# A weighted sum over eight experts: engine code without a block, longer weight runs, and another split of the last eighteen tokens

## The chip, the cores and the metric

The kernel runs on one core of one Trainium2 chip. Its time is the device time of one execution in microseconds; below, "the time" is the median of three executions. One further execution was recorded by the hardware profiler, and all views come from that one.

A core has a tensor engine (PE; its weight loads are shown apart, as PEld), a vector engine (DVE), a scalar engine (ACT), GpSimd (POOL) and SyncE (SP), and 16 DMA engines that serve transfers issued from SP and from ACT. Engines wait for each other through semaphores. An on-chip tensor has 128 partitions.

## The reference

```
# expert_outputs: [16, 1024, 8, 512] float32      combine_weights: [16, 1024, 8] float32
weights = combine_weights[..., np.newaxis]
return np.sum(expert_outputs * weights, axis=2).astype(np.float32)
```

For each of 16,384 tokens, eight vectors of 512 numbers are scaled by eight weights and summed. 268 MB are read and 33.6 MB are written, so each byte that is read is used once.

## The kernel before

Each of the 128 partitions works on 128 tokens of its own. "Token j" below means one token in every partition, so 128 tokens at once; its input is 2 MB and its output 0.25 MB.

**Layout.** The first 120 tokens of a partition come in 12 rounds of R = 10. In a round a partition holds ten neighbouring tokens, that is one block of 160 KB in memory, and the next partition has the next block. The last eight tokens (`x_l`, `w_l`, `o_l`) are eight neighbours per partition. `ring` holds the input of ten tokens on chip, `acc` ten results, `w_t` all weights, `w_c` the weights of the current round.

**The loop.** Rounds 0 to 10 (`ROUNDS` = 11, `LOOP` = 110 tokens) run in a hardware loop on DVE alone. In each pass DVE takes the three chunks of a round (4, 4 and 2 tokens); for each it waits for the copied weights (`w_set`), for the stores that free `acc` (`stored`) and for the load (`loaded`). Then it works on two tokens at a time: a scaled copy for term 0 (L226), and fused multiply-adds for terms 1 to 7 (L230), the two tokens taking turns so that no instruction follows directly on the one whose sum it needs. The last term of a token raises `done`. The argument `head_slot` of the loop sets at which place of an instruction fetch block the loop's first instruction lies.

**The tail.** The last 18 tokens (`TAIL`, j = 0 to 17; the last two are called a and b) are split between PE and DVE. ACT makes diagonal matrices from an identity and a weight (`diag`, L161), 32 of them ahead. PE multiplies such a matrix with a token's input and adds up terms 0 to 3 in one of eight PSUM banks (`ps`, L208). DVE adds terms 4 to 7, still two tokens at a time: its first instruction for a token reads `ps` and waits for `product`, the count of finished products; the others read `acc`.

**Queues.** SP issues all loads in order: weights (L114, L117), the loop's chunks (L122, each after `done` says that its place in `ring` is free), the tail's (L131: two tokens at a time, then single ones, and a and b in pieces of four, two and one term). After the last load SP issues the "held" stores of tokens 10 to 15, a and b (L137), each once DVE has done its tokens; at last it waits for all stores. ACT issues the stores of the loop (L178) and of tokens 0 to 9 (L191), copies weights and makes the diagonals.

**The block.** Every engine's code stands in a function of its own under one `nc.Block()`. The block's entry and its end (L110) are branches of every engine, and its end is a barrier of all engines; a second barrier of the surrounding program follows (L315).

Of the kernel before, what the change touches and what calls it, by code (L numbers as in the profile page):

```python
# [10 lines left out]
def kernel(  # L11
# [16 lines left out]
    nc = tc.nc  # L28
# [5 lines left out]
    P = 128  # L34
    R = 10
    T_P = T // P
    FULL = T_P // R
# [6 lines left out]
    PE_E = 4  # L44
    DIAGS = 8 * PE_E
    BANKS = 8

# [4 lines left out]
    x_r = x[0:cut].rearrange("(n p r) e d -> n p r e d", p=P, r=R)  # L52
    w_r = w[0:cut].rearrange("(n p r) e -> p n r e", p=P, r=R)
    o_r = o[0:cut].rearrange("(n p r) d -> n p r d", p=P, r=R)
    x_l = x[cut:T].rearrange("(p r) e d -> p r e d", r=LAST)
    w_l = w[cut:T].rearrange("(p r) e -> p r e", r=LAST)
    o_l = o[cut:T].rearrange("(p r) d -> p r d", r=LAST)

# [9 lines left out]


    tail_loads = [(j, 2, 0, E) for j in range(0, R, 2)]  # L70
    tail_loads += [(j, 1, 0, E) for j in range(R, TAIL - 2)]
    a, b = TAIL - 2, TAIL - 1
    tail_loads += [(a, 1, 0, 4), (b, 1, 0, 4), (a, 1, 4, 6), (b, 1, 4, 6)]
    tail_loads += [(a, 1, 6, 8), (b, 1, 6, 7), (b, 1, 7, 8)]

    tail_stores = [(0, 4), (4, 4), (8, 2)]
    held_stores = [(R, 6), (a, 1), (b, 1)]
# [15 lines left out]

    def x_tail(j, m, e0, e1):
        if j < R:
            return x_r[ROUNDS, :, j : j + m, e0:e1]
        return x_l[:, j - R : j - R + m, e0:e1]

    def o_tail(j, m):
        if j < R:  # L100
            return o_r[ROUNDS, :, j : j + m]
        return o_l[:, j - R : j - R + m]
# [5 lines left out]

    with tc.tile_critical(no_gpsimd_drain=True):  # L109
        with nc.Block() as block:  # L110

            @block.sync
            def _(sync):
                sync.dma_start(  # L114
                    out=w_t[:, 0 : FULL * R].rearrange("p (n r) e -> p n r e", r=R), in_=w_r
                ).then_inc(w_in, 16)
                sync.dma_start(out=w_t[:, FULL * R : T_P], in_=w_l).then_inc(w_in, 16)  # L117
                for n in range(ROUNDS):
                    for c, (r, m) in enumerate(CHUNKS):
                        if n:  # L120
                            sync.wait_ge(done, (n - 1) * R + r + m)
                        sync.dma_start(  # L122
                            out=ring[:, r : r + m], in_=x_r[n, :, r : r + m]
                        ).then_inc(loaded[c], 16)
                free = 0
                for k, (j, m, e0, e1) in enumerate(tail_loads):
                    if LOOP - R + j + m > free:
                        free = LOOP - R + j + m
                        sync.wait_ge(done, free)
                    r = j % R  # L130
                    sync.dma_start(  # L131
                        out=ring[:, r : r + m, e0:e1], in_=x_tail(j, m, e0, e1)
                    ).then_inc(tail_in[k], 16)
                for j, m in held_stores:
                    r = j % R
                    sync.wait_ge(done, LOOP + j + m)
                    sync.dma_start(out=o_tail(j, m), in_=acc[:, r : r + m]).then_inc(held_out, 16)  # L137
                sync.wait_ge(held_out, 16 * len(held_stores))
                for k in range(len(tail_stores)):
                    sync.wait_ge(tail_out[k], 16)  # L140

            @block.gpsimd
            def _(gpsimd):
                gpsimd.memset(ident, 0.0).then_inc(id_set, 1)  # L144
                gpsimd.affine_select(  # L145
                    out=ident,
                    in_=ident,
                    compare_op=mybir.AluOpType.not_equal,
                    fill=1.0,
                    base=0,  # L150
                    pattern=[[-1, P]],
                    channel_multiplier=1,
                ).wait_op(id_set, 1, "sem-ge").then_inc(id_set, 1)

            @block.scalar
            def _(scalar):
                def diags(j):

                    for e in range(PE_E):
                        k = j * PE_E + e  # L160
                        i = scalar.mul(  # L161
                            out=diag[:, k % DIAGS],
                            in_=ident,
                            mul=w_t[:, LOOP + j, e : e + 1],
                        ).then_inc(diag_set, 1)
                        if k >= DIAGS:
                            i.wait_op(product, k - DIAGS + 1, "sem-ge")

                scalar.wait_ge(w_in, 32)
                for n in range(ROUNDS + 1):  # L170
                    if n == ROUNDS:
                        scalar.wait_ge(id_set, 2)
                        for j in range(DIAGS // PE_E):
                            diags(j)
                    for c, (r, m) in enumerate(CHUNKS):
                        if n:
                            scalar.wait_ge(done, (n - 1) * R + r + m)
                            scalar.dma_start(  # L178
                                out=o_r[n - 1, :, r : r + m], in_=acc[:, r : r + m]
                            ).then_inc(stored[c], 16)  # L180
                        if n < ROUNDS:
                            scalar.copy(  # L182
                                out=w_c[:, r : r + m], in_=w_t[:, n * R + r : n * R + r + m]
                            ).then_inc(w_set[c], 1)
                ahead = DIAGS // PE_E
                for k, (j, m) in enumerate(tail_stores):
                    while ahead < min(TAIL, j + m + 6):
                        diags(ahead)
                        ahead += 1
                    scalar.wait_ge(done, LOOP + j + m)  # L190
                    scalar.dma_start(out=o_tail(j, m), in_=acc[:, j : j + m]).then_inc(  # L191
                        tail_out[k], 16
                    )
                while ahead < TAIL:
                    diags(ahead)
                    ahead += 1

            @block.tensor
            def _(tensor):
                for j in range(TAIL):  # L200
                    if j >= BANKS:
                        tensor.wait_ge(done, LOOP + j - BANKS + 1)
                    for e in range(PE_E):
                        k = j * PE_E + e
                        if e == 0 or load_of(j, e) != load_of(j, e - 1):
                            tensor.wait_ge(tail_in[load_of(j, e)], 16)
                        tensor.wait_ge(diag_set, k + 1)
                        tensor.matmul(  # L208
                            ps[:, j % BANKS],
                            lhsT=diag[:, k % DIAGS],  # L210
                            rhs=ring[:, j % R, e],
                            start=e == 0,
                            stop=e == PE_E - 1,
                        ).then_inc(product, 1)

            @block.vector
            def _(vector):
                def take(s, v):
                    vector.wait_ge(s, v).then_inc(s, -v)  # L219

                count = {}

                def term(r, e, first, weight, before):

                    if before is None:
                        i = vector.tensor_scalar_mul(  # L226
                            out=acc[:, r], in0=ring[:, r, e], scalar1=weight
                        )
                    else:
                        i = vector.scalar_tensor_tensor(  # L230
                            out=acc[:, r],
                            in0=ring[:, r, e],
                            scalar=weight,
                            in1=before,
                            op0=mult,
                            op1=add,
                        )
                    if e > first:
                        i.wait_op(step, count[r], "sem-ge")
                    if e < E - 1:  # L240
                        i.then_inc(step, 1)
                        count["all"] += 1
                        count[r] = count["all"]
                    else:
                        i.then_inc(done, 1)
                    return i

                for c in range(C):
                    vector.sem_inc(stored[c], 16)
                with nc.Fori(  # L250
# [69 lines left out]
```

## Time and profile before

| What | Value |
|---|---|
| time, median of three | 712.41 us (712.12 to 712.58) |
| the profiled execution: its own time, its span | 712.39 us, 710.5 us |
| DVE busy | 604.5 us (85%) |
| PE, PEld, ACT busy | 69.5, 28.4, 30.3 us |
| bytes moved, mean rate | 302.57 MB, 426 GB/s |
| one fused term of 128x512 on DVE | 745 ns |
| one diagonal on ACT, one PE pass | 388 ns, 637 ns (as recorded) |
| issue to landing of a tail load (L131), median | 36.6 us |

The span goes from the first recorded instruction to the last; the rest of the time lies around it. Busy time is that of an engine's own instructions; semaphore, branch and DMA-issuing instructions are not counted. Durations overlap where an engine is pipelined: a fused term is recorded with 745 ns, but six in a row take 4.06 us, and a matrix product of float32 shows as two passes. A row of the chain of waits names what released each step, followed back from the end.

### The profile page before, as it was taken

The numbers are of one execution on the slowest core, as the hardware profiler recorded it, in microseconds if no ns is written. First come the engines' busy times: TensorE is split into PE (matmuls) and PEld (weight loads), VectorE is DVE, ScalarE is ACT, GpSimd is POOL, SyncE is SP. The second block draws the span as 40 slices with busy tenths as digits, with TensorE's granted clock in tenths as the row PEclk, the third lists the DMA queues.
The fourth block names the chain that finished last, engine by engine and source line by source line (L and its number), as shares of the span: only waits on it lengthen the run. The fifth ranks groups of instructions, "written<-read, shape, count | busy, mean of one in ns | idle before, by whom it ended". The sixth has DMA issues, their size and how long they took to land. (4 is left out here: it accounts for less than half of the span.)

```text
span 710.5 us, 1687 instructions
## 1 busy us (share of the span) xinstructions
PE 69.5 (10%) x144; PEld 28.4 (4%) x144; DVE 604.5 (85%) x952; ACT 30.3 (4%) x106; POOL 0.7 (0%) x6
## 2 busy tenths in 40 slices
PE   0000000000000000000000000000000000567775
PEld 0000000000000000000000000000000000222322
DVE  0599899899899899899899899899899899954555
ACT  0000000000000000000000000000000140021200
POOL 0000000000000000000000000000000000000000
PEclk9999999999999999999999999999999999998998
DMA  9999999999999999999999999999999999999996
GB/s 381 421 420 461 410 422 438 452 405 467 409 427 437 457 405 462 404 439 429 455 415 448 415 436 439 438 421 443 445 408 456 422 447 410 424 441 425 429 425 247
DMA packets 14661, 302.57 MB, mean 426 GB/s; under 512 B 3136, under 2 KB 3136, under 8 KB 5568
## 3 DMA queue, kind: packets, MB, share of 16 engines
q1 hardware_dynamic: 9472, 271.06, 88.6%
q10 hardware_dynamic: 5184, 31.46, 10.5%
q14 instruction: 4, 0.03, 0.0%
q8 instruction: 1, 0.02, 0.0%
HBM read 268.96 MB, written 33.55 MB: 426 GB/s over the span
## 5 line engine op out<-in xcount | busy, mean ns | idle before, releaser
L230 DVE SCALAR_TENSOR_TENSOR acc<-ring,w_c,acc 128x512 f32<-128x512 f32 x770 | 514.7, 745 | 0.0
L208 PE MATMUL ps<-ring,diag 128*128 128x512 f32 x144 | 69.5, 637 | 632.2 <-DMA ring<-in_expert_outputs_dram 621.6
L226 DVE TENSOR_SCALAR acc<-ring,w_c 128x512 f32<-128x512 f32 x110 | 48.3, 481 | 64.5 <-DVEq L219 64.5
L208 PEld LDWEIGHTS ps<-ring,diag 128*128 128x128 f32 x144 | 28.4, 203 | 672.5 <-DMA ring<-in_expert_outputs_dram 624.1
L230 DVE SCALAR_TENSOR_TENSOR acc<-ring,w_t,ps 128x512 f32<-128x512 f32 x18 | 13.4, 746 | 37.4 <-PE ps L208 37.4
L230 DVE SCALAR_TENSOR_TENSOR acc<-ring,w_t,acc 128x512 f32<-128x512 f32 x54 | 36.5, 746 | 0.0
L182 ACT COPY w_c<-w_t 128x32 f32<-128x32 f32 (+1 forms) x33 | 6.8, 213 | 557.2 <-DVE acc L230 554.0
L161 ACT ACTIVATE diag<-ident,w_t 128x128 f32<-128x128 f32 x72 | 22.2, 388 | 84.6 <-PE ps L208 77.0
L182 ACT ACT_TABLE_LOAD x1 | 1.3, 1283 | 0.9 <-SPq L109 0.9
L145 POOL TENSOR_SCALAR_AFFINE_SELECT ident<-ident 128x128 f32<-128x128 f32 x1 | 0.3, 292 | 0.1
L144 POOL MEMSET ident<- 128x128 f32 x1 | 0.2, 204 | 0.5 <-SPq L109 0.5
L304 POOL MEMSET const-bfloat16-1.0<- 128x1 bf16 x1 | 0.1, 102 | 0.0
L304 POOL MEMSET const-uint8-127<- 128x1 uint8 x1 | 0.1, 102 | 0.0
L304 POOL MEMSET const-float32-0.0<- 128x1 f32 x1 | 0.1, 99 | 0.2 <-issue 0.2
L304 POOL MEMSET const-float32-1.0<- 128x1 f32 x1 | 0.1, 99 | 0.0
## 6 DMA issues: line engine op xcount, KB each, us to landing
ring<-in_expert_outputs_dram SPq DMA_DIRECT2D x16, 4096.0 KB, 35.4
out_dram<-acc ACTq DMA_DIRECT2D x24, 1024.0 KB, 26.8
ring<-in_expert_outputs_dram SPq DMA_DIRECT2D x6, 2048.0 KB, 41.2
out_dram<-acc ACTq DMA_DIRECT2D x12, 512.0 KB, 30.8
ring<-in_expert_outputs_dram SPq DMA_DIRECT2D x2, 1024.0 KB, 35.0
ring<-in_expert_outputs_dram SPq DMA_DIRECT2D x3, 512.0 KB, 36.8
out_dram<-acc SPq DMA_DIRECT2D x1, 1536.0 KB, 5.2
ring<-in_expert_outputs_dram SPq DMA_DIRECT2D x2, 256.0 KB, 27.8
```

What stands on the lines that cost most here:

```text
L144: gpsimd.memset(ident, 0.0).then_inc(id_set, 1)
L145: gpsimd.affine_select(out=ident, in_=ident, compare_op=mybir.AluOpType.not_equal, fill=1.0, base=0, pattern=[[-1, P]], channel_multiplier ...
L161: i = scalar.mul(out=diag[:, k % DIAGS], in_=ident, mul=w_t[:, LOOP + j, e : e + 1],).then_inc(diag_set, 1)
L182: scalar.copy(out=w_c[:, r : r + m], in_=w_t[:, n * R + r : n * R + r + m]).then_inc(w_set[c], 1)
L208: tensor.matmul(ps[:, j % BANKS], lhsT=diag[:, k % DIAGS], rhs=ring[:, j % R, e], start=e == 0, stop=e == PE_E - 1,).then_inc(product, 1)
L226: i = vector.tensor_scalar_mul(out=acc[:, r], in0=ring[:, r, e], scalar1=weight)
L230: i = vector.scalar_tensor_tensor(out=acc[:, r], in0=ring[:, r, e], scalar=weight, in1=before, op0=mult, op1=add,)
L304: nc = _bacc.Bacc("TRN2", target_bir_lowering=False, num_devices=1)
```

## The change

- Each engine's code is a plain function, called one after the other, without a block; the loop has no `head_slot`.
- A partition holds 20 neighbouring tokens over two rounds (index h), so its weights come in runs of 640 bytes instead of 320. x and the output are read and written by the same map: a round's block of 160 KB is now 320 KB from the next partition's.
- PE sums two terms of tokens 0 to 7, three of tokens 8 to 15, and four of a and b (`pe_e`): 48 products instead of 72, and 24 more terms on DVE. 36 diagonals are made ahead instead of 32.
- DVE takes tokens 14 and 15 one after the other, each term upon its own token's last, and a and b in the order a4 a5 a6 b4 a7 b5 b6 b7.
- The held store of six tokens is split into four and two.
- SP's closing waits stand in another order.

```
-    x_r = x[0:cut].rearrange("(n p r) e d -> n p r e d", p=P, r=R)
-    w_r = w[0:cut].rearrange("(n p r) e -> p n r e", p=P, r=R)
-    o_r = o[0:cut].rearrange("(n p r) d -> n p r d", p=P, r=R)
+    x_r = x[0:cut].rearrange("(n p h r) e d -> n h p r e d", p=P, h=2, r=R)
+    w_r = w[0:cut].rearrange("(n p g) e -> p n g e", p=P, g=G)
+    o_r = o[0:cut].rearrange("(n p h r) d -> n h p r d", p=P, h=2, r=R)
...
+    a, b = TAIL - 2, TAIL - 1
+    pe_e = [2] * 8 + [3] * (TAIL - 10) + [4, 4]
...
-    held_stores = [(R, 6), (a, 1), (b, 1)]
+    held_stores = [(R, 4), (R + 4, 2), (a, 1), (b, 1)]
+
+    order = []
+    for q in range(0, TAIL - 4, 2):
+        order += [(j, e) for e in range(pe_e[q], E) for j in (q, q + 1)]
+    for j in (TAIL - 4, TAIL - 3):
+        order += [(j, e) for e in range(pe_e[j], E)]
+    order += [(a, 4), (a, 5), (a, 6), (b, 4), (a, 7), (b, 5), (b, 6), (b, 7)]
+
+    diags = [(j, e) for j in range(TAIL) for e in range(pe_e[j])]
+    DIAGS = 36
...
+    def weights_and_stores(scalar):
+        made = 0
+
+        def make(end):
+            nonlocal made
+            for k in range(made, min(end, len(diags))):
+                j, e = diags[k]
+                i = scalar.mul(
+                    out=diag[:, k % DIAGS], in_=ident, mul=w_t[:, LOOP + j, e : e + 1]
+                ).then_inc(diag_set, 1)
+                if k >= DIAGS:
+                    i.wait_op(product, k - DIAGS + 1, "sem-ge")
+            made = max(made, end)
...
+        for k, (j, m) in enumerate(tail_stores):
+            make(len([1 for i, e in diags if i < j + m]) + DIAGS // 2)
+            scalar.wait_ge(done, LOOP + j + m)
+            scalar.dma_start(out=o_tail(j, m), in_=acc[:, j : j + m]).then_inc(tail_out[k], 16)
+        make(len(diags))
...
-                with nc.Fori(
-                    0, ROUNDS, engines=OrderedEngineSet([vector.engine]), head_slot={vector.engine: 0}
-                ):
+        with nc.Fori(0, ROUNDS, engines=OrderedEngineSet([vector.engine])):
...
+        for j, e in order:
+            r = j % R
...
+            weight = w_t[:, LOOP + j, e : e + 1]
+            if e == pe_e[j]:
+                i = fused(r, e, weight, ps[:, j % BANKS])
+                i.wait_op(product, sum(pe_e[: j + 1]), "sem-ge")
+            else:
+                i = fused(r, e, weight, acc[:, r])
+                i.wait_op(step, last[r], "sem-ge")
+            count(i, r, e)
...
     with tc.tile_critical(no_gpsimd_drain=True):
-        with nc.Block() as block:
+        loads_and_held_stores(nc.sync)
+        identity(nc.gpsimd)
+        weights_and_stores(nc.scalar)
+        first_terms(nc.tensor)
+        terms(nc.vector)
```

## The prediction

> **What bounds the kernel now.** I read the page's slices first, then its DMA parts, then the stage table of the end, then the chain, then the sequencers' rows at both ends.
>
> ```profile
> span 710.5 us, 1687 instructions
> ...
> DVE  0599899899899899899899899899899899954555
> ...
> DMA  9999999999999999999999999999999999999996
> ...
> DMA packets 14661, 302.57 MB, mean 426 GB/s; under 512 B 3136, under 2 KB 3136, under 8 KB 5568
> ...
> q14 instruction: 4, 0.03, 0.0%
> ...
> L226 DVE TENSOR_SCALAR acc<-ring,w_c 128x512 f32<-128x512 f32 x110 | 48.3, 481 | 64.5 <-DVEq L219 64.5
> ```
>
> The DMA row is nine tenths or more in 39 of 40 slices: transfers bound the kernel from the first microseconds almost to the end. DVE looks as full, but has idle time: 64.5 us at L226 (a wait, L219, for loads), 25.75 of it before the first load lands, so 38.7 in the ten later passes, about 3.9 a pass. A microsecond saved on DVE inside the loop is worth nothing; one taken off the transfers, or off what follows the last load, counts in full. The stage table (PE, PEld, DVE, ACT, POOL busy, clock, DMA share, GB/s) shows where that begins:
>
> ```profile
> 690.00:695.00 5.00, 3.86 (x9) 1.82 (x10) 0.83 (x2) 0.00 (x0) 0.00 (x0) 1.00 1.00 412
> 695.00:700.00 5.00, 5.00 (x13) 2.28 (x12) 5.00 (x8) 0.00 (x0) 0.00 (x0) 1.00 0.69 267
> 700.00:705.00 5.00, 1.68 (x4) 0.38 (x2) 3.51 (x6) 0.00 (x0) 0.00 (x0) 0.96 0.76 317
> 705.00:710.50 5.50, 0.00 (x0) 0.00 (x0) 1.44 (x3) 0.00 (x0) 0.00 (x0) 0.50 0.26 98
> ```
>
> DMA is full to about 698, then falls to 0.69. The chain of waits names what holds the end:
>
> ```profile
> 686.22 3.67 PE ps L208 x8
> 689.90 1.24 issue
> 691.14 10.55 PE ps L208 x24
> 701.69 0.03 issue
> 701.72 0.81 DVE acc L230 x2
> ```
>
> PE works 10.55 us without a gap on the last three tokens (15, a=16, b=17), four terms of 0.857 us each (two passes), and DVE cannot begin b before 701.72. Timeline rows of DVE and SP show the rest:
>
> ```profile
> 699.49 0.74 DVE L230 SCALAR_TENSOR_TENSOR acc<-ring,w_t,ps 128x512 f32<-128x512 f32 x1
> 699.60 7.20 SPq L137 DMA_DIRECT2D out_dram<-acc  x3
> ...
> 701.72 0.75 DVE L230 SCALAR_TENSOR_TENSOR acc<-ring,w_t,ps 128x512 f32<-128x512 f32 x1 [1.49 <-PE ps L208]
> 702.38 4.06 DVE L230 SCALAR_TENSOR_TENSOR acc<-ring,w_t,acc 128x512 f32<-128x512 f32 x6
> ```
>
> Six interleaved terms take 4.06 us, 0.663 from start to start; the last ends at 706.44, its store lands at 708.50. From there to the end of the span (2.0 us) only sequencers run. Load semaphores add one fact: the last load's 15th count comes at 699.30, the 16th at 701.10. One DMA engine is behind. It is 0.86 behind at the first load already, and 1.8 from 658 on. The instruction queue's four 8 KB reads start at 2.70 (0.82 us long), 9.68, 538.9 and 651.9 (0.31 each); by the packet records those at 2.70 and 9.68 are on the late engine.
>
> **The change, part by part.** The profiled execution took 712.39 us (span 710.5 plus 1.9 around it), the median is 712.41: I use the sum as it is on the median.
>
> *Weights.* 1,536 runs of 320 bytes become 768 of 640. The packet records give 20.6 ns for 320 bytes (1.98 us over 16 engines), 18 for 256, 84 for 2 KB: about 9 ns plus 37 per KB, so 32 ns for 640 bytes, 1.54 us. Saved 0.45, ahead of the first x load on the same queue, with the DMA full afterwards: it shifts every landing. [...] The rows here lie on one straight line through 256 and 320 bytes: I take 0.45.
>
> *The other grouping of tokens.* x, weights and output use the same new token map; a partition's next block is 320 KB away instead of 160. Packet counts and sizes of x do not change. Before, blocks 160 KB apart run at 2.418 us per 64 KB packet, and those of the last eight tokens, 128 KB apart, at 0.611 per 16 KB: the same line. I take 0. Bounds: -1 to +3 us, if HBM minds the distance (0.4% of the stream).
>
> *Block gone, at the start.* SP's branch at 0.80 is followed by its first DMA at 0.955. I take 0.1 of that (0 to 0.15). At the end, a whole barrier goes. SP's row after the last landing is L110 at 708.52, L109 begins at 708.89: 0.37, of which I count 0.3 (0.2 to 0.4), since a branch stays.
>
> *No fixed head for the DVE loop.* The fetch at 2.70 came right after DVE's branch into its aligned loop. Without the alignment DVE runs straight on, and one or two of its three reads (2.70, 9.68, 651.9) should go. That engine's lag of 1.8 would shrink to 0.6 to 1.8; I take a gain of 0.6 (0 to 1.2). What else can happen is the rival below.
>
> *TensorE sums 2 or 3 terms instead of 4.* 24 products go: 24 x 0.857 = 20.6 us of PE, 24 x 0.29 of ACT (both idle beside it), and DVE gets 24 x 0.663 = 15.9 us more. Over tokens 0 to 9 a pair arrives every 11.5 us; DVE needs 12 x 0.663 = 8.0 after PE's two short sums (3.6): 11.6 from landing to done, as against 13.6 now (646.5 to 660.1). The first pair is later (628 instead of 625.3), as DVE leaves the loop only at 620; what waits for that is SP's load of tokens 10 and 11, which today lands 37 us after its issue behind a full queue: no cost; without that queue it would be 2.7 us. ACT makes 36 weights ahead instead of 32, 1.2 us between stores that wait for DVE anyway.
>
> *The last tokens.* With today's landings: product of 13 at 681.24 + 2.85 = 684.1; ten interleaved terms of 12/13 carry DVE to 690.1. Token 14 is now alone, so each term waits for the one before. No such pair is in the trace. Below it is 0.745 (duration) and above 0.9; I take 0.78 (0.745 + 0.01 to the semaphore + 0.03 to the start, as from PE's 701.69 to 701.72). Five terms, four of those gaps and one of 0.663: 3.8 us. Token 14: 690.1 to 693.9; token 15 (product at 691.14 + 2.8) 694.0 to 697.8. a: two terms from 697.75, the third when its load lands (699.8). PE ends token 15 at 693.7, a at 697.15, b at 700.6 with its tail 700.8, instead of 701.69: b's first term 700.85, then a's last 701.5, b's 702.2, 703.0, 703.75, end 704.5. Against 706.44: 1.95 saved. With 0.9 for a dependent term it is 1.5.
>
> *Held stores.* The 1.5 MB store (landed 704.8) becomes 1 MB after token 13 and 0.5 MB after 15. The first is issued near 690, behind all loads on the same queue, so it delays none; it fills the gap after 698. Sum on the late engine: 700.6 + 2.4 + 1.2 + 0.65 = 704.9 before b's store, whose first packet comes about 1.1 us after its issue (705.6 at the earliest): no cost, with 0.7 of cover. One DMA issue more on SP (0.34) lies near 690.
>
> Sum: 0.45 + 0.1 + 0.6 + 1.95 + 0.3 = 3.4; landings move earlier together with PE and DVE, so these add, but a's third load and b's sum must both move: I round to 3.2. 712.4 - 3.2 = **709.2**.
>
> **Rivals.**
>
> *Only the tail and barrier gain (no lag recovered, dependent terms at 0.9):* 0.45 + 1.5 + 0.3 = 2.2: 710.2. For it: the lag jumped at 651.9 and may do so again.
>
> *The loop is fetched again on each pass: slower.* The loop is 92 instructions (80 terms, 10 waits, 2 to close). Today it sits at the head of a fetch block, and between 9.7 and 538.9 not one fetch occurs. [...] It decides from four extra reads' worth upward: ten reads (3.1) cancel the gain. I give 0.15 to the full form, 0.08 to one read per pass (712.3).
>
> *HBM minds the new distance:* 0.03, 714 to 716.
>
> **How the numbers follow.** Main case 0.60 (708.0 to 710.4), small gain 0.14 (710 to 711.4), one read per pass 0.08, full refetch 0.15, HBM 0.03. This kernel's measurement tells about 0.2% (1.4 us) from no change: faster below 711.0. Faster 0.60 + 0.11 = 0.71, same 0.03 + 0.08 = 0.11, slower 0.18. The range 708.0 to 713.0 leaves out the full refetch, HBM and a little below.
>
> **What would show it.** First x packets near 3.5 instead of 3.9; 16th count of the last load at 700 instead of 701.1; queue 14 with two or three reads, not dozens; PE's last run ending near 699.5; SP's last store issued near 703 with about 1.7 us to the span's end after it lands. Wrong: more than ten reads on q14, L226 idle well above 64.5, or a mean DMA rate in 100 to 500 us below that of before.

## The result, and the profile after

The changed kernel took 711.17 us (median of four, 710.61 to 711.55), the kernel before 712.45 us beside it: a ratio of 0.9982, interval 0.9965 to 0.9999. So 1.3 us, 0.18%, were gained where 3.2 were forecast. The profiled execution took 710.61 us; its span is 708.4, so 2.2 us lie around it. From the page after:

```profile
span 708.4 us, 1576 instructions
...
DVE  0599899899899899899899899899899989996777
...
PEclk9999999999999999999999999999999999976888
DMA  9999999999999999999999999999999999999997
...
DMA packets 14035, 302.54 MB, mean 427 GB/s; under 512 B 1616, under 2 KB 2384, under 8 KB 4944
...
q14 instruction: 3, 0.02, 0.0%
...
L245 DVE TENSOR_SCALAR acc<-ring,w_c 128x512 f32<-128x512 f32 x110 | 48.3, 481 | 65.8 <-DVEq L215 65.8
```

The loop is not fetched again on its passes: queue q14 has three reads instead of four, the idle time at the loop's wait is 65.8 us instead of 64.5, the DMA row is as full as it was. That rules out the rival by which the loop is fetched again on each pass. Two lines are new. The granted clock of PE falls to 0.6 and 0.7 in slices near the end, and the line `q8 instruction: 1, 0.02, 0.0%`, which stands on the page before, is gone. Both turn out to matter. The stage table (PE, PEld, DVE, ACT, POOL busy, clock, DMA share, GB/s) and then the chain of waits after:

```profile
690.00:695.00 5.00, 4.60 (x12) 1.85 (x11) 4.34 (x7) 0.00 (x0) 0.00 (x0) 0.99 1.00 414
695.00:700.00 5.00, 5.00 (x13) 2.20 (x12) 4.82 (x7) 0.00 (x0) 0.00 (x0) 1.00 1.03 412
700.00:705.00 5.00, 1.08 (x3) 0.19 (x1) 4.52 (x7) 0.00 (x0) 0.00 (x0) 0.88 0.63 256
```

```profile
686.50 4.51 PE ps L205 x6
691.01 0.40 issue
691.41 9.69 PE ps L205 x22
701.10 0.02 issue
701.12 0.82 DVE acc L229 x2
```

The DMA engines are now busy between 695 and 700 (share 1.03, before 0.69): the earlier held store fills the gap. PE's last run has 22 passes in 9.69 us (24 in 10.55 before). But the run ahead of it, six passes of token 14, took 4.51 us; six passes at full rate take 2.81 (a row further below). DVE's and SP's rows of the end:

```profile
699.44 1.54 DVE L229 SCALAR_TENSOR_TENSOR acc<-ring,w_t,acc 128x512 f32<-128x512 f32 x2
701.12 0.75 DVE L229 SCALAR_TENSOR_TENSOR acc<-ring,w_t,ps 128x512 f32<-128x512 f32 x1
701.79 2.98 DVE L229 SCALAR_TENSOR_TENSOR acc<-ring,w_t,acc 128x512 f32<-128x512 f32 x4
```

```profile
702.56 2.57 SPq L144 DMA_DIRECT2D out_dram<-acc  x2
```

DVE ends at 704.77 (before 706.44) and the last store lands at 706.81 (before 708.50).

Three quantities are followed through all runs below: when the first load of x is complete (16th count; 25.62 before, 26.28 after), how long the span goes on after the last load has landed (710.46 - 701.10 = 9.36 before; 708.39 - 701.35 = 7.04 after), and the time outside the span, which is a run's time less its span.

### The profile page after: what moved, and what is told of

The parts are those of the page before. It is cut to its first block, busy times and chain, and to the rows that moved or that the text cites. A ratio compares the mean times of both kernels' runs of the same rounds, so it can differ in the third digit from the quotient of the medians.

```text
span 708.4 us, 1576 instructions
## 1 busy us (share of the span) xinstructions
PE 58.8 (8%) x96; PEld 22.7 (3%) x96; DVE 621.2 (88%) x976; ACT 22.4 (3%) x82; POOL 0.7 (0%) x6
## 5 line engine op out<-in xcount | busy, mean ns | idle before, releaser
L205 PE MATMUL ps<-ring,diag 128*128 128x512 f32 x96 | 58.8, 772 | 642.3 <-DMA ring<-in_expert_outputs_dram 629.4
L245 DVE TENSOR_SCALAR acc<-ring,w_c 128x512 f32<-128x512 f32 x110 | 48.3, 481 | 65.8 <-DVEq L215 65.8
L229 DVE SCALAR_TENSOR_TENSOR acc<-ring,w_t,acc 128x512 f32<-128x512 f32 x78 | 53.4, 747 | 0.4
L205 PEld LDWEIGHTS ps<-ring,diag 128*128 128x128 f32 x96 | 22.7, 248 | 677.5 <-DMA ring<-in_expert_outputs_dram 632.0
L168 ACT ACTIVATE diag<-ident,w_t 128x128 f32<-128x128 f32 x48 | 14.3, 391 | 93.9 <-DVE acc L229 93.9
```

What stands on the lines that cost most here:

```text
L168: i = scalar.mul(out=diag[:, k % DIAGS], in_=ident, mul=w_t[:, LOOP + j, e : e + 1]).then_inc(diag_set, 1)
L205: tensor.matmul(ps[:, j % BANKS], lhsT=diag[:, k % DIAGS], rhs=ring[:, j % R, e], start=e == 0, stop=e == pe_e[j] - 1,).then_inc(product, 1)
L229: return vector.scalar_tensor_tensor(out=acc[:, r], in0=ring[:, r, e], scalar=weight, in1=before, op0=mult, op1=add)
L245: i = vector.tensor_scalar_mul(out=acc[:, k], in0=ring[:, k, 0], scalar1=weight)
```

## The experiments

In the first eight the change is taken apart from both ends. Each was timed against the kernel before on the same chip; ratios are to that.

**The changed kernel again** (no edit).

> The changed kernel once more, to see how much of its start varies from run to run. In its first profile the last of the 16 DMA engines ended the first load at 26.28 us (before: 25.62) and the last load at 701.35 (before: 701.10). If the late start belongs to the kernel, the first landing is again 26.0 or later and the time 710.6 to 711.6. If it was one execution's accident, the first landing is near 25.0 and the time near 710.

**The old token map** in it, with weights in 320-byte runs:

```
+    x_r = x[0:cut].rearrange("(n h p r) e d -> n h p r e d", p=P, h=2, r=R)
+    w_r = w[0:cut].rearrange("(n p r) e -> p n r e", p=P, r=R)
```

> The changed kernel with the token map of before (weights in 320-byte runs, blocks 160 KB apart); block, loop, tail and stores as changed. Theory D (distance: engines that read 64 KB blocks 320 KB apart disturb each other at the start): first landing 25.3 or earlier, last landing near 700.2, time near 710.0, about 1.1 below the changed kernel. Theory W (the shorter weight phase only uncovers a start that the x reads need anyway, so 0.45 us become idle): first and last landing as in the changed kernel, time within 0.3 of it.

**The old map with 640-byte runs** (the weights that arrive belong to other tokens):

```
+    x_r = x[0:cut].rearrange("(n h p r) e d -> n h p r e d", p=P, h=2, r=R)
     w_r = w[0:cut].rearrange("(n p g) e -> p n g e", p=P, g=G)
```

> The changed kernel with x and output in the map of before, but the weights still read in 640-byte runs, so each result is made with another token's weights; all instructions and transfers are there. Theory D: this one has the gain of both, first landing 25.0 or earlier and time 0.4 below e_oldmap. Theory W: the x reads start no earlier, first landing 26.0 or later, time as the changed kernel.

**The new map with 320-byte runs**, in two loads:

```
+    w_r = w[0:cut].rearrange("(n p h r) e -> h p n r e", p=P, h=2, r=R)
+        for h in range(2):
+            sync.dma_start(out=w_o[h], in_=w_r[h]).then_inc(w_in, 16)
```

> The changed kernel with its map of x and output, but the weights of the rounds read in 320-byte runs by two DMAs (one more DMA issue of about 0.45 us on SP, behind which the x loads are issued later). Theory D: the late start is that of the map, first landing 26.3 to 26.8, time as the changed kernel or up to 0.5 more. Theory W: with the longer weight phase the x reads start together again, first landing near 25.3 and time near 710.

**The kernel before with the new tail and stores only** (block and old map kept; SP's closing waits stand in the new order):

```
+    pe_e = [2] * 8 + [3] * (TAIL - 10) + [4, 4]
+    held_stores = [(R, 4), (R + 4, 2), (a, 1), (b, 1)]
```

> The kernel before with the new split of the last eighteen tokens alone (two to four terms on TensorE, order, smaller held stores); block, fixed loop head and token map as before. Span: 1.9 to 2.0 less than before (710.1), that is 708.2, as predicted for the tail. Time outside the span (before: 2.0 in every execution; the changed kernel: 2.1 or 3.1): theory P (TensorE's shorter code moves a code fetch behind the end) expects 2.1 or 3.1 here; theory B (it comes from the block's removal) expects 2.0 always, and a time of 710.2.

**The kernel before with the block and head_slot taken away only:**

```
-        with nc.Block() as block:
+        if True:
...
-                    0, ROUNDS, engines=OrderedEngineSet([vector.engine]), head_slot={vector.engine: 0}
+                    0, ROUNDS, engines=OrderedEngineSet([vector.engine])
```

> The kernel before without the block and without the fixed loop head, nothing else changed. Span: 0.4 less for the barrier, and up to 0.8 less if the engine that fetched code at 2.70 and 9.68 us was what held each load back: 709.0 to 709.7. Time outside the span: theory P expects 2.0 always, theory B 2.1 or 3.1, so that the time (712.25) hardly falls.

**The kernel before with the new map and 640-byte weights only:**

```
+    x_r = x[0:cut].rearrange("(n p h r) e d -> n h p r e d", p=P, h=2, r=R)
+    w_r = w[0:cut].rearrange("(n p g) e -> p n g e", p=P, g=2 * R)
```

> The kernel before with the new token map and the 640-byte weight runs alone. As predicted: span 0.45 less. Theory W, now with uncovered starts of the x reads: the last engine ends the first load near 26.3 instead of 25.6 and the span is the same or up to 0.7 longer. Time outside the span 2.0 in both theories.

**The changed kernel with the block and head_slot put back:**

```
+        with nc.Fori(0, ROUNDS, engines=OrderedEngineSet([vector.engine]), head_slot={vector.engine: 0}):
...
+        with nc.Block() as block:
+            block.sync(loads_and_held_stores)
+            block.gpsimd(identity)
+            block.scalar(weights_and_stores)
+            block.tensor(first_terms)
+            block.vector(terms)
```

> The changed kernel with the block and the fixed loop head put back. Span: 0.4 more for the barrier than the changed kernel's (707.4 to 709.7, mostly 707.5 or 709.1), plus up to 0.8 if the code fetches near 2.7 and 9.7 us return and delay one engine: 708 to 709.5. Time outside the span: theory P 2.1 or 3.1, theory B 2.0 always.

| kernel | time, median us | ratio, 95% | spans us | outside, mean us (runs over 2.6) | first load complete in its profile |
|---|---|---|---|---|---|
| changed, again | 710.78 | 0.9982 (0.9973 to 0.9990) | 707.4 to 709.7 | 2.82 (8 of 11) | 26.32 |
| changed, old map, 320 | 710.39 | 0.9977 (0.9969 to 0.9986) | 706.6 to 708.7 | 2.89 (9 of 11) | 25.16 |
| changed, old map, 640 | 711.94 | 0.9986 (0.9977 to 0.9995) | 707.3 to 709.4 | 2.89 (9 of 12) | 26.28 |
| changed, new map, 320 | 711.09 | 0.9981 (0.9972 to 0.9990) | 707.0 to 709.2 | 2.80 (7 of 11) | 25.91 |
| before + tail | 711.75 | 0.9989 (0.9980 to 0.9999) | 708.0 to 710.2 | 2.57 (5 of 10) | 26.35 |
| before - block | 710.64 | 0.9974 (0.9965 to 0.9984) | 708.2 to 709.7 | 2.02 (0 of 10) | 25.12 |
| before + map | 712.44 | 0.9998 (0.9989 to 1.0008) | 710.2 to 710.7 | 2.01 (0 of 10) | 26.53 |
| changed + block | 712.42 | 0.9991 (0.9981 to 1.0000) | 708.0 to 710.1 | 2.58 (4 of 10) | 26.59 |

What follows. The new map with its weights is worth nothing by itself. Taking the block away, always together with head_slot, is worth 1.7 us in the mean, no less than the whole change (the two intervals overlap); which of the two it is was not taken apart. The new tail alone, without that, gives 0.7 us in the median (712.48 beside it). And the tail brings two things: spans in two groups (706.6 to 709.9 over the 37 executions of the changed kernel, half of them near 707.7 and half near 709.2; the kernel before has 709.7 to 711.6), and, in more than half of the changed kernel's runs, about 1 us more outside the span. The kernel before was outside for over 2.6 us in none of its 130 runs beside these experiments. Putting the block back does not take this away, and removing it from the kernel before does not bring it, so theory B is out.

Of the theories on the late first load, D (distance) expected 25.0 or earlier for the old map with 640-byte runs, and it was 26.28. W expected 26.0 or later there and about 26.3 for the new map alone, and 26.28 and 26.53 came; but for the new map with 320-byte runs it expected 25.3, and 25.91 came. The times of these kernels differ too little to decide.

First the spans. Of the changed kernel, run once more at the end of the study, the rows of PE (start, duration, passes, idle time before):

> The changed kernel itself, on the same chip as f_long: spans of 707.3 to 709.9 in two groups, 2.0 or about 3 us outside, 710.8, ratio 0.998. If f_long's gain over it is real, the two intervals of the ratio do not overlap.

```profile
685.71 2.81 PE L205 MATMUL ps<-ring,diag 128*128 128x512 f32 x6 [2.04 <-issue]
690.60 11.38 PE L205 MATMUL ps<-ring,diag 128*128 128x512 f32 x22 [2.08 <-DVE acc L229]
```

This is the same last run of 22 passes that took 9.69 us above. From 692.0 to 695.4, 1.4 us into the run, the granted clock is halved and the passes start 0.857 us apart instead of 0.43, so token b's sum and the end come 1.7 us later: the span goes on for 8.74 us after the last landing. The run measured 712.36 us in the median, ratio 0.9988 (0.9978 to 0.9999), spans 706.6 to 709.6, over 2.6 us outside in 8 of 11.

Such losses of the clock can be counted in all 20 profiles. Between two of PE's runs in the tail (after 640 us) lies a pause; a run of PE counts as slow if a pass of half rate is among its first four. The pause is counted from 0.43 us after the start of the last pass ahead of it, which gives 0.15 or so more than the idle column above:

| pause before the run of PE | runs | slow |
|---|---|---|
| under 2.15 us | 44 | 0 |
| 2.15 to 2.5 us | 24 | 8 |
| 2.5 to 3 us | 11 | 7 |
| 3 to 4 us | 11 | 10 |
| over 4 us | 29 | 29 |

With four terms a token, PE pauses 1.1 to 1.4 us ahead of token 15's products; with three, mostly 2.2 to 2.3. The next runs test whether this is the cause, and what the time outside the span depends on. TensorE's code has 330 instructions before and 222 in the changed kernel. In the packet records of the kernels with 72 products, a read of 16 KB on the instruction queue q8 starts 0.4 to 0.6 us ahead of the end of the span; with 48 it comes 1.7 to 2.3 us behind it in six of nine profiles, and in three it is not recorded.

**Empty instructions on TensorE:**

```
+        for k in range(108):
+            tensor.nop()
```

> The changed kernel with 108 empty instructions at the start of TensorE's stream, where TensorE waits for the tail anyway; they bring TensorE's code back to about its length before. Theory P (the tail kernels' longer time outside the span comes from TensorE's shorter code, by which a read of instructions on queue q8 falls behind the last instruction): that read is back inside the span, 0.4 to 0.6 us before its end, the time outside is 2.0 us in every run instead of 2.0 or 2.9, the span is as in the changed kernel (707.4 to 709.7), the median time about 709.9 against 710.8. Rival (the lengths of ScalarE's or VectorE's code do it, or it is not the code's length at all): the time outside stays at 2.0 in some runs and 2.9 or more in most, the time at 710.8.

The compiler leaves empty instructions out (TensorE's code has 222 again), so this was the changed kernel's own code: 710.79 us, 0.9981 (0.9972 to 0.9991), spans 707.3 to 709.9, over 2.6 us outside in 6 of 11. It says nothing of the theory and counts as one more repetition.

**Unused products in the tail:**

```
+            if e == 0:
+                for q in range(2 if j >= BANKS else 1):
+                    tensor.matmul(
+                        ps[:, j % BANKS], lhsT=ident, rhs=w_t[:, 0:64], start=True, stop=True
+                    )
```

> The changed kernel with products that nobody uses: one ahead of each of the first eight tail tokens' products, two ahead of each later token's, of the identity and 512 columns of the weights, into the bank that the token's first product then overwrites. The output is the reference's. Theory of the clock (TensorE's slow passes of 0.857 us come from its longer idle stretches): the bursts from the eighth token on run at 0.43 us a pass in every profile, the last run of 22 passes takes about 9.7 us, the span loses its upper length of 709.1 to 709.7 and stays at 707.4 to 707.8; with the code longer again (24 products' worth, theory P) the time outside is 2.0, so the time is 709.4 to 709.9. Rival (the slow passes come from outside the kernel, or the extra products only push the real ones back): slow passes remain or the last burst ends later, the span is 708 to 709.7, the time 710.5 or more.

712.87 us, 1.0008 (0.9999 to 1.0017): a miss. No late pass is slow, but the chain shows what I had overlooked (L205 are the unused products, L212 the token's own):

```profile
692.71 1.72 PE ps L205 x4
694.42 3.43 PE ps L212 x8
697.86 1.72 PE ps L205 x4
699.57 3.45 PE ps L212 x8
703.02 0.02 issue
```

The extra products ahead of a and b lie on the path: 3.4 us. The time outside, however, was 2.04 us in the mean and never over 2.3.

**The same in the old map with 320-byte weights.**

> The changed kernel without the block, with the split of the tail, the stores and the unused products of d_warm, but with the old assignment of tokens to partitions and the weights in 320-byte runs. If the three causes add up (start 0.4 to 0.6 earlier without the 640-byte runs, no slow passes in the last burst, 2.0 outside): first load complete at 25.1, span 706.7 to 707.2, time 708.7 to 709.2, ratio 0.995, below every kernel so far. If the start does not matter (the loads catch up later): span 707.4, time 709.4. If slow passes come back: 710 or more.

712.76 us, 1.0005 (0.9996 to 1.0014), first load complete at 25.08, 2.05 outside: the same fault in the tail hides the rest.

**The weights issued by ScalarE** in the kernel just above (both loads of them), so that SP issues x at once:

```
+        scalar.dma_start(
+            out=w_t[:, 0 : FULL * R].rearrange("p (n r) e -> p n r e", r=R), in_=w_r
+        ).then_inc(w_in, 16)
```

> f_best with the two loads of the weights issued by ScalarE instead of SyncE, so that the first load of x is issued by SyncE at 0.95 instead of 2.24 us. If the start of x is held by its place behind the weights in SyncE's issues, x packets start about 1 us earlier, the first load is complete 0.3 to 0.6 earlier (24.6), and the time falls by as much, to 708.3 to 708.8. Rival (the engines' work is the limit, the weights' packets take their 1.98 us of the 16 engines wherever they are issued): the first load is complete at 25.1 again and the time is that of f_best; if the two queues share each engine packet by packet, the weights land later than 4.8 us, which costs nothing, as they are first used at 25.

735.98 us, 1.0335 (1.0321 to 1.0350). x does start early (first packet at 1.97) and its first load is complete at 23.41. But neither theory had the weights landing after 50 us (row of the DMA issues: queue, KB, us to landing):

```profile
w_t<-in_combine_weights_dram ACTq DMA_DIRECT2D x1, 480.0 KB, 52.6
```

```profile
GB/s 402 413 357 0 379 443 397 446 450 414 423 449 421 453 412 438 462 420 419 446 450 402 434 450 443 396 446 450 443 395 448 450 421 422 425 437 426 429 425 252
```

The weights land at about 54 us, when the three loads that fill the ring are through. Until then DVE has no weights; then the ring is full, DVE has everything still to do, and for a whole slice nothing moves. The packet records show how: by 50 us, 368 packets of x (2.42 us for 64 KB) and 384 of the 1,536 small weight packets (0.02 us each) have started, one small for one large; the rest of the 1,536 have all started by 53.5 us, as x runs out. I had assumed a delay of a few microseconds.

Four further runs put the extra work where it is not on the path.

**One unused product ahead of tokens 8 to 15, none for a and b:**

```
+            if e == 0 and BANKS <= j < a:
+                tensor.matmul(
+                    ps[:, j % BANKS], lhsT=ident, rhs=w_t[:, 0:64], start=True, stop=True
+                )
```

> The changed kernel with one product that nobody uses ahead of the products of each of the tail's tokens 8 to 15, none ahead of the last two tokens (d_warm had put two ahead of every later token, 3.4 us of them between the last two tokens' own products). TensorE then has 8 passes a token there, as the kernel before has. Theory of the clock: these bursts run at 0.43 us a pass, the last run of 22 passes takes 9.5 to 9.7 us in the profile, the span's upper length of 709 and more is gone, the span is 707.3 to 707.8 in every run. The time outside, by theory P (long TensorE code keeps it at 2.0): TensorE's code is 254 instructions here (222 in the changed kernel, 330 before, 334 in d_warm), so it is 2.0 if the length decides steadily, 2.0 or 2.9 as before if a length over 256 is needed. Time 709.5 or 710.2. Rival (slow passes do not come from idle time): spans 707.4 to 709.7 as in the changed kernel, time 710.8.

**24 unused products at the start of TensorE's code:**

```
+        for q in range(24):
+            tensor.matmul(ps[:, 0], lhsT=ident, rhs=w_t[:, 0:64], start=True, stop=True)
```

> The changed kernel with 24 unused products in a row at the start of TensorE's stream, 650 us ahead of the tail: TensorE's code is 319 instructions again (d_pad's empty instructions were left out by the compiler, so d_pad ran the changed kernel's own code), and nothing in the tail is different. Theory P (code length): 2.0 us outside the span in every run, the span as in the changed kernel with its two lengths, 707.4 to 709.7; time 709.5 to 711.2, median 710.0. Rival (the time outside comes from the tail's shape on TensorE, which d_warm also changed): outside 2.0 or 2.9 as in the changed kernel, time 710.8.

**Four real terms on TensorE from token 8 on:**

```
+    pe_e = [2] * 8 + [4] * (TAIL - 8)
```

> The changed kernel with four terms of every token from the eighth on summed on TensorE, in place of three (the last two have four already): 56 products, 8 passes a token, and 8 terms fewer on VectorE. Theory of the clock: warm as d_warm2, and VectorE done earlier with tokens 12 to 15, but the end is set by the last burst on TensorE (24 passes now for the last three tokens, from the landing of token 15 at 690.4): 10.4 us, so the last product ends at about 700.8 if TensorE runs from there without a pause, the span is 708.2 to 708.4, and steady; time 710.2 to 711. If the clock does not matter, the span has two lengths, 708.5 and 710 or more.

**Old map, 320 bytes, four terms from token 8 on, three for a:**

```
+    pe_e = [2] * 8 + [4] * (TAIL - 10) + [3, 4]
+    order += [(a, 3), (a, 4), (a, 5), (b, 4), (a, 6), (b, 5), (a, 7), (b, 6), (b, 7)]
```

> The old assignment of tokens and 320-byte weights, no block, the changed tail with four terms on TensorE for tokens 8 to 15 and the last token, three for the last but one (its fourth term is the first on VectorE). TensorE: token 15's 8 passes, then 6, then 8: if warm they end at 699.0 to 699.9, bounded by the last token's first load at 695.4 and by 22 passes from 690. VectorE has one more term at the end but is free earlier: last term from 702.3 to 702.9, in e_oldmap 703.01. Span 706.7 to 707.3 and steady, time 708.7 to 709.3 with 2.0 outside, 709.6 to 710.2 with 2.9. Rival (VectorE's one more term is on the path): span 707.8 or more, time 710 or more.

| kernel | time, median us | ratio, 95% | spans us | outside, mean us (runs over 2.6) | TensorE's code |
|---|---|---|---|---|---|
| one unused product, 8 to 15 | 710.23 | 0.9969 (0.9958 to 0.9980) | 707.8 to 709.3 | 2.12 (0 of 7) | 254 |
| 24 at the start | 710.70 | 0.9976 (0.9967 to 0.9986) | 707.0 to 709.5 | 2.12 (0 of 10) | 319 |
| four terms from 8 on | 711.30 | 0.9983 (0.9974 to 0.9992) | 706.8 to 708.7 | 3.07 (10 of 11) | 254 |
| old map, four terms | 710.21 | 0.9966 (0.9952 to 0.9980) | 707.0 to 708.1 | 2.49 (2 of 5) | 250 |

The kernel with 24 products at the start differs from the changed one in nothing but TensorE's code, 650 us ahead of the tail, and all its ten runs have 1.99 to 2.23 us outside. That shows that TensorE's code makes the difference, and not the shape of the tail. Its page has the read on q8 again (it starts at 660.25, inside the span):

```profile
q8 instruction: 1, 0.02, 0.0%
```

Its spans still have both lengths, as expected, since its tail pauses as before. But 254 instructions kept the time outside at 2.1 in one kernel and not in another, so the length alone does not decide. The place of this read fits better: in all 20 profiled executions the time outside is 1.8 to 2.2 us where the read lies inside the span (9) or is not recorded (4), and 2.5 to 3.3 us where it comes behind the end (7). Whether the read holds up the end, and what in the code places it, stays open.

On the pauses: in the three kernels of this table that shorten them, the pause ahead of token 15's products is 1.36 to 1.39 us and no run of PE after 675 us is slow. With four real terms the spans stay below 708.8 in all 16 runs. One prediction failed in part: with one unused product a span of 709.3 remained, the profiled one. There no pass is slow, and the span goes on for 6.96 us after the last landing as it should; its last load landed at 702.39, against 699.6 to 701.9 in the profiles of the other kernels (the one with the weights on ScalarE aside).

The same kernel with 24 products at the start shows the clock directly. Its first products end at 27.90 us; after that PE has nothing to do. Stretches, PE's busy time, the granted clock, DMA share, GB/s:

```profile
24.00:28.00 4.00, 3.90 (x10) 1.00 0.64 279
28.00:30.00 2.00, 0.00 (x0) 1.00 1.21 524
30.00:32.00 2.00, 0.00 (x0) 1.00 1.21 524
32.00:34.00 2.00, 0.00 (x0) 0.81 1.13 492
34.00:40.00 6.00, 0.00 (x0) 0.50 0.83 360
```

The clock is halved 4 to 6 us after the last product.

The traces settle why a pause of one length is slow at one time and not at another. In all 20 profiles every stretch of one granted clock, but for the last, is a whole multiple of 3.41 us long. From 600 us on, cut each trace into such windows and add up the passes in each (0.43 us a pass, 0.855 at half rate). After a full-rate window in which PE was busy for less than 0.36 of the time, the next is at half rate (106 of 106); from 0.41 on it never is (0 of 251); in between it is in 5 of 12. After a half-rate window the next is at full rate if PE was busy for 0.79 or more (91 of 91, below that 0 of 103). In the slow run above, the window from 688.6 is busy for 0.39 and the next is at half rate; in the old map with 640-byte runs the pause ahead of token 15 is as long, but it lies so that the window from 689.1 is busy for 0.43, and the clock stays. So, as an estimate from these numbers, the shortest pause that can cost the clock is about 0.63 x 3.41 = 2.15 us, one of twice that always does, and between them it depends on where the pause lies in the windows. The pause of 1.4 us that four terms a token leave ahead of token 15 is too short wherever it lies.

**Everything together:** the last kernel with the 24 products at the start.

```
     pe_e = [2] * 8 + [4] * (TAIL - 10) + [3, 4]
+        for q in range(24):
+            tensor.matmul(ps[:, 0], lhsT=ident, rhs=w_t[:, 0:64], start=True, stop=True)
```

> f_four with d_long's 24 unused products at the start of TensorE's stream (TensorE's code 347 instructions in place of 250). If the parts add up: span as f_four's, 707.0 to 708.1, median 707.3, and 2.0 to 2.2 us outside it in every run as with d_long: 709.4, ratio 0.9958, below every kernel so far. Rival (the length that kept the time outside at 2.0 does not do so here, as 254 instructions did in d_warm2 and not in d_four): 2.0 or 3.0 outside, 710.0 as f_four.

It took 709.94 us (709.81 to 710.20 in five runs), 0.9966 (0.9952 to 0.9980), with spans of 707.7 to 708.1 and 1.8 to 2.2 us outside. The chain:

```profile
685.65 3.67 PE ps L209 x8
689.32 1.22 issue
690.54 9.69 PE ps L209 x22
700.23 0.03 issue
```

Its time outside and its steadiness came as expected; its span is 0.7 longer than expected, its first load complete at 26.10 in spite of 320-byte weights. It is 0.3% faster than the kernel before, clear of noise. Against the changed kernel run beside it the medians differ by 2.4 us, yet the intervals of the two ratios still overlap, by 0.0002, and the changed kernel's fastest run (708.78) is below it. So it is the steadier one; that it is faster in general is likely and not shown.

## Why the prediction was wrong

The forecast was 709.2 us; over 37 executions the changed kernel's mean is 711.17, the kernel before's is 712.39 over 130. Of the 1.22 between them, 1.91 is span (710.35 to 708.44) and -0.69 is time outside (2.05 to 2.73). Against 3.2, then, 1.3 is missing in the span and 0.7 was given back outside. The step that failed most is the one that took 24 products from TensorE at no price ("both idle beside it"): it brought the halved clock, up to 0.75 us of the mean span, and the 0.7 outside. The rest of what is missing is close to the weights' 0.45, which did not come. By the steps of the sum:

- **Weights, 0.45: failed.** SP issues x earlier (2.02 instead of 2.24 us). But a packet of 640 bytes took 35 ns in this profile and 37 to 41 in the other ten that have them, not 32, and the last of these packets ends at 4.00 to 5.17 us, 4.40 in the mean of the eleven; with 320 bytes it is 4.13 to 4.85, 4.34 in the mean of eight. So the weights were hardly done sooner. The start "with the DMA full afterwards" was not full either: the 16 earliest packets of x start at 3.61 to 5.37 in the changed kernel's profile, the last four of them from 4.65 on (before, 3.88 to 4.33, one at 4.85). The first load was complete at 26.06 in the mean of eleven profiles with 640-byte weights (24.16 to 26.74), at 25.58 in eight with 320 (25.08 to 26.35). The gain is absent; whether there is a loss of 0.5 is not settled, and why some of x's packets start late was not found.
- **Block at the start, 0.1: failed.** The first DMA is issued at 0.952 us instead of 0.955.
- **Barrier, 0.3: at the low end of its range.** From the last store's landing to the end of the span it is 1.58 us instead of 1.96: 0.38. But taking away the block gives only 0.20 of it (1.96 to 1.76, and with the new tail 1.79 to 1.58); the rest came with the new tail and its order of closing waits (1.96 to 1.79), for which the sum had no term.
- **The late engine, 0.6: a gain of this kind, but its cause is not shown.** Without the block and head_slot the reads of q14 at 2.70 and 9.68 go, and one at about 50 us comes; with both put back they are there again (3.78 and 10.63). Taking both away in the kernel before brings the last load from 701.10 to 699.58, its 16th count only 0.13 behind the 15th; with the end's 0.25 that is the 1.7 us measured. But the lag does not follow these reads: with the new map alone they are there (3.53 and 9.87) and the counts end 0.04 apart, and in the kernel with one unused product they are gone and the counts end 1.77 apart. In the changed kernel's profile the counts are 0.57 apart instead of 1.80, and yet the last load is at 701.35.
- **The tail, 1.95: right at full clock, and the largest miss where it is not.** At full clock the part after the last load's landing shrank by 9.36 - 7.04 = 2.32, less the 0.38 of the end: 1.94. The dependent term, taken at 0.78, takes 0.787. What failed is "24 x 0.857 = 20.6 us of PE, 24 x 0.29 of ACT (both idle beside it)": I gave the removed products no price. They had kept the pause ahead of the last run at 1.4 us; without them it is 2.2, and where the clock falls the last run takes 11.4 us instead of 9.7, which takes back 1.7 of the 1.95. About half of the 37 spans are of the longer kind, 709.2 against 707.7 in the mean; if all of these are slow last runs, as both profiles of the changed kernel over 709 us showed, that is 0.75 of the missing 1.3. A late last load can lengthen a span as well, as the 709.3 above shows, so this is an upper figure.
- **Time outside the span: left out.** "span 710.5 plus 1.9 around it" was taken over unchanged. It grew by 0.7 with TensorE's code 108 instructions shorter, and 24 unused products at its start took 0.6 of that back.

The map (0) held: 0.9998 with its weights alone. The held stores (0) were not tested by themselves; the DMA engines are full to 700 with them. The loop was not fetched again: no run shows the reads on each pass to which 0.15 and 0.08 were given; in the changed kernel's profile q14 has three reads in the span, at 51.71, 539.66 and 692.99 us. The first rival, 710.2, came nearest, but by luck: in the profile the lag did shrink, and the dependent term was 0.787 and not 0.9.

## What to carry to other kernels

Work that is taken off an idle engine is not free if it kept that engine's clock up (here the lower clock took back 1.7 of the tail's 1.95 us): look at the pauses between PE's runs, in the chain's "issue" rows, and keep those ahead of a last run well below 2 us (here none of 44 runs of PE was slow after a pause under 2.15, and 1.4 was always short enough), best with real work. Add up the whole time and not the span: read the time outside it in several runs, and whether the read of instructions on q8 is still inside. A kernel whose runs have two lengths needs as many profiles as it has lengths; one profile of the changed kernel would have shown the tail's full gain and nothing of its price.

## What the runs showed of the hardware that was not expected

- PE's passes of 0.43 us took 0.857 after pauses as short as 2.19 us, never below 2.15 (44 cases), always above 4 us (29 cases). In all 20 profiles the clock was granted in windows of 3.41 us: after a full-rate window busy for less than 0.36 the next was at half rate (106 of 106), from 0.41 on never (0 of 251).
- With shorter TensorE code the time outside the span was longer: 222 instructions in place of 330, and 2.73 us in the mean in place of 2.05; 24 unused products 650 us before the tail put it back to 2.12. With 254 instructions it was 2.12 in one kernel and 3.07 in another.
- 480 KB of weights in 320-byte packets on ACT's queue took 52.6 us beside 64 KB packets on SP's, one small packet for each large one; on SP's queue ahead of them, 3.5 us.
